# Queries computed by channels and rotated in that form, in a Mamba-2 and sliding-window attention trunk

## The chip, the cores and the metric

The kernel runs on one core of a Trainium2 chip. The metric is device time in microseconds for one launch. Before the change the median of three runs is 982.54 us (981.25 to 983.72). The trace shown below is of one more execution, which took 981.03 us.

## What is computed

The reference is a trunk of two layers on 256 tokens of 2048 channels, in float32. The first layer is a Mamba-2 mixer, the second a sliding-window attention. The change lies in the second layer alone, cut here to what matters:

```python
def _rope_partial(x, cos, sin):          # head dimension 64, the first 16 channels turn in pairs (i, i + 8)
    x1, x2, rest = xf[..., :8], xf[..., 8:16], xf[..., 16:]
    out = jnp.concatenate([x1 * cos - x2 * sin, x2 * cos + x1 * sin, rest], axis=-1)

def _swa_mixer(x, k, v, cos, sin, w_in, q_bias, sinks, w_out):
    proj = x @ w_in                                       # 256 x 2048 by 2048 x 4096
    q = (proj[..., :2048] + q_bias).reshape(1, 256, 4, 8, 64)
    gate = proj[..., 2048:]
    q = _rope_partial(q, ...)
    o = _swa_sink_attention(q, k, v, sinks)               # 4 key heads, 8 query heads each, window 128
    return (o * jax.nn.silu(gate)) @ w_out
```

The layer's output is added to the scaled input and normalised over the channels.

## The kernel before

**Products.** Every large product is made of three: a float32 operand is split into a rounded part (`wh`, `x1H`) and the rest (`wl`, `x1L`), and high by high, high by low and low by high are summed in one PSUM bank. Weights come from HBM in units of 128 x 2048 (two loads of 512 KB on SyncE's queue). ScalarE writes a unit's `wh` (L164) and VectorE its `wl` (L167), each in two halves of 1024 columns. There are four buffers for `wh` and four for `wl`, so a new unit's ScalarE piece has to wait until TensorE has read the unit four before it.

**Two forms.** In the form by tokens (`x_stat`, L1006) a tile of the input, 128 channels by 128 tokens, is stationary and 512 weight columns move; tokens come out on the partitions. One weight unit takes 24 such products, 12 for each half of the tokens. In the form by channels (`mac`, L252) a 128 x 128 tile of weights is stationary and all 256 tokens move; channels come out on the partitions. One weight unit takes 48 such products. In this second form a weight tile may lie *broken*: its first 128 columns apart from the rest, at another offset in the buffer (`BROKEN`, `BROKEN2`), and then the first half is written in two pieces.

**The second layer.** After keys and values (`kv`, form by tokens, two groups of transposes, L1063, turn the keys), twelve blocks of four weight units follow in the order of `B_ORDER`: query blocks `q` 0 to 3 (one key head each, 512 channels), gate blocks `g` 0 to 3 (form by channels), and output blocks `o` 0 to 3 (L323 to L325, 512 columns moving). Units of this layer are counted here from the first of `q` 0, so that `q` 0 is units 1 to 4, `g` 0 units 5 to 8, `q` 1 9 to 12, `g` 1 13 to 16, `q` 2 17 to 20, `o` 0 21 to 24, `g` 2 25 to 28, `q` 3 29 to 32, `o` 1 33 to 36, `g` 3 37 to 40, `o` 2 and `o` 3 after that.

**What runs between units.** `tick()` is called after each unit. `later(n, fn)` puts a piece of work on TensorE's list n units later. So a query block's transposes (`qtr`) come two units after it, its attention scores (`attend`, L1139 for the first 128 tokens) three units after it, the scores of the second half (L1146) three units later, and the products with the values (L1249, or L1263 and L1270) some units after those.

**A query block.** Two PSUM tiles, one for each half of the tokens, are filled over four units. VectorE adds the bias row (L1090, a row of 512 that GpSimd loads and spreads over the partitions, L981), turns the 16 rotary channels of each head (`rope`, six small operations, L991 to L996), TensorE transposes the 128 x 512 result into a PSUM tile (L1096, four transposes), and ScalarE copies it out with the factor 1/8 (L1100).

The engines run their own lists in order; within them the order comes from the program and a scheduler. ScalarE also makes the gates' tanh (L1116), the exponentials (L1174) and the moves of 32 x 256 pieces (L1207). VectorE also transposes the probabilities in 32 x 32 pieces (L1188) and applies the first layer's gains to the residual (L1028, L1029).

Of the kernel before, what the change touches and what calls it, by code (L numbers as in the profile page):

```python
# [8 lines left out]
F32 = mybir.dt.float32  # L9
# [74 lines left out]
def trunk(ctx: ExitStack, tc: tile.TileContext, A: dict, out: bass.AP, dbg=None):  # L84
    nc = tc.nc
# [8 lines left out]
    cst = pool("cst")  # L94
# [108 lines left out]
    srcs = []  # L203
# [11 lines left out]
    srcs += wo_srcs("wo", NG - 1) + [A["wkv"][i] for i in range(4)]  # L215
    places = {}
    for what, j in B_ORDER:
        if what == "g":

            places.update({len(srcs) + i: BROKEN2 if (i, j) == (1, 0) else BROKEN for i in range(4)})  # L220
        srcs += wo_srcs({"q": "wq", "g": "wg", "o": "wb"}[what], j)
    units = []
    used = [0]
# [34 lines left out]
    def later(n, fn, place=None):  # L258
        pending.insert(len(pending) if place is None else place, [n, fn])
# [528 lines left out]

    cs = cst.tile([P, 2, 8], F32, tag="cs", name="cs")
    sn = cst.tile([P, 2, 8], F32, tag="sn", name="sn")  # L790

    def rotary():
        posi = ap.tile([P, 2], I32, tag="posi", name="posi")
        tc.keep_in_program_order(nc.gpsimd.dma_start(posi[:], A["pos"]))
        inv = ap.tile([P, 8], F32, tag="inv", name="inv")
        tc.keep_in_program_order(nc.gpsimd.dma_start(inv[:], A["inv"]))
        posf = ap.tile([P, 2], F32, tag="posf", name="posf")
        nc.vector.tensor_copy(posf[:], posi[:])
        ang = ap.tile([P, 2, 8], F32, tag="ang", name="ang")
        nn = ap.tile([P, 2, 8], F32, tag="nn", name="nn")  # L800
        for h in range(2):
            nc.vector.tensor_scalar(ang[:, h, :], inv[:], posf[:, h : h + 1], None, ALU.mult)
        nc.vector.tensor_scalar(nn[:], ang[:], 1.0 / TWO_PI, None, ALU.mult)
        nc.vector.tensor_scalar(nn[:], nn[:], ROUND, None, ALU.add)
        nc.vector.tensor_scalar(nn[:], nn[:], ROUND, None, ALU.subtract)
        for c in (CW1, CW2, CW3):
            nc.vector.scalar_tensor_tensor(ang[:], nn[:], -c, ang[:], ALU.mult, ALU.add)
        nc.scalar.activation(sn[:], ang[:], AF.Sin)
        sh = ap.tile([P, 2, 8], F32, tag="sh", name="sh")
        nc.scalar.activation(sh[:], ang[:], AF.Sin, scale=0.5)  # L810
        nc.vector.tensor_tensor(sh[:], sh[:], sh[:], ALU.mult)
        nc.vector.tensor_scalar(cs[:], sh[:], -2.0, 1.0, ALU.mult, ALU.add)


    plan = {}
# [163 lines left out]
    def bias_row(src):  # L979
        t = bp.tile([P, 512], F32, tag="bias", name=nm("bias"), bufs=1)  # L980
        nc.gpsimd.dma_start(t[:], src.partition_broadcast(P))  # L981
        return t

    def rope(v, h, n):

        c = cs[:, h : h + 1, :].to_broadcast([P, n, 8])
        s = sn[:, h : h + 1, :].to_broadcast([P, n, 8])
        t = bp.tile([P, 4, 8, 8], F32, tag="rt", name=nm("rt"), bufs=1)
        x1, x2 = v[:, :, 0:8], v[:, :, 8:16]
        a, b, d, e = [t[:, i, :n, :] for i in range(4)]  # L990
        nc.vector.tensor_tensor(a, x1, c, ALU.mult)  # L991
        nc.vector.tensor_tensor(b, x2, s, ALU.mult)
        nc.vector.tensor_tensor(d, x2, c, ALU.mult)
        nc.vector.tensor_tensor(e, x1, s, ALU.mult)
        nc.vector.tensor_tensor(x1, a, b, ALU.subtract)
        tc.keep_in_program_order(nc.vector.tensor_tensor(x2, d, e, ALU.add))  # L996

    def x_stat(ps, h, u, ui, pin=False, last=None):

        todo = [(k, i) for k in range(4) for i in range(3) if i != last]  # L1000
        todo += [(k, last) for k in range(4) if last]
        for k, i in todo:
            kk = ui * 4 + k
            ks = slice(k * 512, (k + 1) * 512)
            hs = slice(h * P, (h + 1) * P)
            m = nc.tensor.matmul(  # L1006
                ps[:], (x1H, x1L, x1H)[i][:, kk, hs], (u.h, u.h, u.l)[i][:, ks],
                start=(kk, i) == (0, 0), stop=ui == 3 and (k, i) == todo[-1],
            )
            pinned(m, pin)  # L1010
# [19 lines left out]

    kT = bp.tile([P, 4, S], F32, tag="kT", name="kT")
    vt = bp.tile([P, 2, S], F32, tag="vt", name="vt")
    kvb = bias_row(A["kvb"])
    kv_u = []
    for h in range(2):
        ps = mm_tile()
# [34 lines left out]
    for i, n in enumerate(RES_AT):  # L1071
        later(n, lambda i=i: residual(i // 2, i % 2))

    qT = {}
    sg = {}
    os_ = {}
    still = []

    def q_block(j):
        pss = [mm_tile(), mm_tile()]  # L1080
        qb = bias_row(A["qb"][j * 512 : (j + 1) * 512])
        for ui in range(4):
            u = next_unit()
            for h in range(2):
                x_stat(pss[h], h, u, ui)
            tick()
        for h in range(2):
            qt = bp.tile([P, 8, 64], F32, tag="qt", name=nm("qt"), bufs=2)
            qf = qt[:].rearrange("p a d -> p (a d)")
            nc.vector.tensor_tensor(qf, pss[h][:], qb[:], ALU.add)  # L1090
            rope(qt[:], h, 8)

            def qtr(h=h, qf=qf):
                pt = ax_tile()
                for p_ in range(4):
                    nc.tensor.transpose(  # L1096
                        pt[:, p_ * P : (p_ + 1) * P], qf[:, p_ * P : (p_ + 1) * P], ident
                    )
                q2 = bp.tile([P, 4, P], F32, tag="qT", name=nm("qT"), bufs=2)
                nc.scalar.activation(  # L1100
                    q2[:], pt[:].rearrange("p (a t) -> p a t", a=4), AF.Copy, scale=0.125
                )
                qT[j, h] = q2

            later(2, qtr)

    def gate_block(j):
        t = bp.tile([P, 4, S], F32, tag="sg", name=nm("sg"), bufs=2)
# [12 lines left out]
    def attend(j, h):  # L1121

        nk = P * (h + 1)
        q2 = qT[j, h]
# [7 lines left out]
        for b in range(0, 4, per):  # L1132
            pss = [ax_tile(), ax_tile()]
            for i in range(per):
                for part in range(h + 1):
                    for par in range(2):
                        rows = slice(64 * par, 64 * par + 64)
                        if h == 0:
                            nc.tensor.matmul(  # L1139
                                pss[par][:, i * nk : (i + 1) * nk], q2[rows, b + i, :], kT[rows, j, :nk],  # L1140
                                start=True, stop=True,
                            )
                            continue

                        qs, at = slice(64 * part, 64 * part + 64), i * nk
                        nc.tensor.matmul(  # L1146
                            pss[par][qs, at : at + 192], q2[rows, b + i, qs],
                            kT[rows, j, 64 * part : 64 * part + 192], start=True, stop=True,
                        )
# [240 lines left out]
def _layout(inputs):  # L1390
# [44 lines left out]
    a["wkv"] = xstat(f["kv_w"], 4, 512)  # L1435
    a["kvb"] = f["kv_b"]
    wi = f["b_w_in"][0]
    a["wq"] = xstat(wi[:, :D], 4, 512)
    a["wg"] = wstat(wi[:, D:])
    a["qb"] = f["b_q_bias"][0]  # L1440
    a["snk"] = f["b_sinks"][0].reshape(4, 4, 2).transpose(0, 2, 1).reshape(32)
    wb = f["b_w_out"][0]
    a["wb"] = xstat(wb, 4, 512).reshape(4, 4, P, 2048).transpose(1, 0, 2, 3).reshape(16, P, 2048)
# [42 lines left out]
```

## Time and profile before

| | |
|---|---|
| median of the three runs | 982.54 us |
| profiled execution, its own time | 981.03 us |
| its span in the trace | 979.0 us |
| TensorE clock granted | 1.00 |
| bytes read from HBM | 195.49 MB, 202 GB/s over the span with the 2.23 MB written |
| keys and values begin, `q` 0 begins, `o` 2 begins | 655.59, 679.21, 923.59 us |

The profile counts a matmul as busy from its start to the modelled end of its flow through the array, and the next starts long before that end. So a row's duration (0.28 us for 256 columns) is no price. The price of a stretch is the distance from its first start to the next stretch's first start. A row of the timeline reads: start, duration, engine, line, operation, output and inputs, stationary and moving shapes, and how many operations were merged. `x1H` and `x1L` are the input of the second layer, `wh` and `wl` a weight unit, `mm` and `ax` PSUM tiles, `qt` the queries by tokens, `qT` the queries by channels, `kT` the keys by channels.

### The profile page before, as it was taken

The numbers are of one execution on the slowest core, as the hardware profiler recorded it, in microseconds if no ns is written. First come the engines' busy times: TensorE is split into PE (matmuls) and PEld (weight loads), VectorE is DVE, ScalarE is ACT, GpSimd is POOL, SyncE is SP. The second block draws the span as 40 slices with busy tenths as digits, with TensorE's granted clock in tenths as the row PEclk, the third lists the DMA queues.
The fourth block names the chain that finished last, engine by engine and source line by source line (L and its number), as shares of the span: only waits on it lengthen the run. The fifth ranks groups of instructions, "written<-read, shape, count | busy, mean of one in ns | idle before, by whom it ended". The sixth has DMA issues, their size and how long they took to land.

```text
span 979.0 us, 18089 instructions
## 1 busy us (share of the span) xinstructions
PE 973.5 (99%) x7012; PEld 884.5 (90%) x7012; DVE 783.3 (80%) x1201; ACT 660.7 (67%) x1222; POOL 98.7 (10%) x137
## 2 busy tenths in 40 slices
PE   9999999999999999999999999999999999999998
PEld 8999989999999998999999999888898878978976
DVE  7898898967888877886887787889867778766786
ACT  7595776764984865776576487566467777764772
POOL 0001303003003002100300300303000000000003
PEclk9999999999999999999999999999999999999999
DMA  9788577764665766666566565458645546564642
GB/s 356 267 289 305 171 223 230 237 201 145 222 221 173 258 207 190 217 202 206 187 212 204 170 203 199 152 166 291 214 153 175 181 162 187 166 210 142 203 142 86
DMA packets 61557, 198.89 MB, mean 203 GB/s; under 512 B 6848, under 2 KB 11360, under 8 KB 61216
## 3 DMA queue, kind: packets, MB, share of 16 engines
q1 hardware_dynamic: 58528, 188.53, 58.6%
q0 software_dynamic: 2336, 8.69, 2.7%
q8 instruction: 55, 0.90, 0.4%
q10 hardware_dynamic: 608, 0.52, 0.2%
q14 instruction: 30, 0.25, 0.1%
HBM read 195.49 MB, written 2.23 MB: 202 GB/s over the span
## 4 chain that ended last, share of the span: by engine, by line
PE 99%; DVE 0%; DVEq 0%; issue 0%
PE mm L252 54%; PE mm L1006 11%; PE mm L323 9%; PE mm L324 9%; PE mm L325 9%; PE ax L654 2%; PE ax L1146 1%; PE ax L1139 0%; PE ax L591 0%; PE mm L390 0%; PE ax L1263 0%; PE ax L1249 0%; PE ax L1096 0%; PE ax L937 0%; PE ax L372 0%; DVE t L1323 0%
## 5 line engine op out<-in xcount | busy, mean ns | idle before, releaser
L167 DVE TENSOR_TENSOR wl<-wr,wh 128x1024 fp32r<-128x1024 f32 (+2 forms) x338 | 392.9, 1180 | 87.9 <-ACT wh L164 84.5
L164 ACT ACTIVATE wh<-wr 128x1024 fp32r<-128x1024 f32 (+2 forms) x338 | 331.4, 1011 | 123.6 <-PE mm L252 63.2
L252 PE MATMUL mm<-xH,wh 128*128 128x256 f32 x1280 | 355.0, 277 | 0.0
L252 PE MATMUL mm<-xL,wh 128*128 128x256 f32 x1280 | 354.0, 277 | 0.0
L252 PE MATMUL mm<-xH,wl 128*128 128x256 f32 x1280 | 353.9, 276 | 0.0
L252 PEld LDWEIGHTS mm<-xH,wh 128*128 128x128 f32 x1280 | 240.6, 188 | 1.8 <-ACT wh L198 0.5
L252 PEld LDWEIGHTS mm<-xL,wh 128*128 128x128 f32 x1280 | 240.6, 188 | 1.0
L252 PEld LDWEIGHTS mm<-xH,wl 128*128 128x128 f32 x1280 | 240.4, 188 | 0.0
L323 PE MATMUL mm<-wh,yH 128*128 128x512 f32 x256 | 101.2, 395 | 0.0
L324 PE MATMUL mm<-wh,yL 128*128 128x512 f32 x256 | 99.8, 390 | 0.0
L325 PE MATMUL mm<-wl,yH 128*128 128x512 f32 x256 | 99.7, 389 | 0.0
L670 POOL TENSOR_TENSOR yz<-yz,z 128x256 f32<-128x256 f32 x32 | 26.8, 846 | 469.4 <-DVE yz L665 469.4
L494 DVE SCALAR_TENSOR_TENSOR cv<-mm,pc,cv 128x255 f32<-128x255 f32 x144 | 68.7, 477 | 5.2 <-ACT cv L492 2.6
L252 PE MATMUL mm<-x1H,wh 128*128 128x256 f32 x256 | 71.9, 281 | 0.0
L252 PE MATMUL mm<-x1L,wh 128*128 128x256 f32 x256 | 71.1, 278 | 0.0
L252 PE MATMUL mm<-x1H,wl 128*128 128x256 f32 x256 | 71.0, 278 | 0.0
L1006 PE MATMUL mm<-wh,x1H 128*128 128x512 f32 x160 | 63.1, 394 | 0.0
L1006 PE MATMUL mm<-wl,x1H 128*128 128x512 f32 x160 | 61.8, 389 | 0.0
L1006 PE MATMUL mm<-wh,x1L 128*128 128x512 f32 x160 | 60.9, 390 | 0.0
L323 PEld LDWEIGHTS mm<-wh,yH 128*128 128x128 f32 x256 | 48.1, 188 | 10.3 <-DVE z L584 0.9
L325 PEld LDWEIGHTS mm<-wl,yH 128*128 128x128 f32 x256 | 48.1, 188 | 10.2
L324 PEld LDWEIGHTS mm<-wh,yL 128*128 128x128 f32 x256 | 48.1, 188 | 9.0
(232 smaller groups left out, 1418.3 us busy)
## 6 DMA issues: line engine op xcount, KB each, us to landing
wr<-in_wa SPq DMA_DIRECT2D x154, 512.0 KB, 5.2
wr<-in_wo SPq DMA_DIRECT2D x64, 512.0 KB, 4.5
wr<-in_wq SPq DMA_DIRECT2D x32, 512.0 KB, 4.6
wr<-in_wg SPq DMA_DIRECT2D x31, 512.0 KB, 5.2
wr<-in_wb SPq DMA_DIRECT2D x16, 512.0 KB, 4.3
wr<-in_wb SPq DMA_DIRECT2D x32, 256.0 KB, 3.8
rb<-rscr SPq DMA_DIRECT2D x11, 512.0 KB, 5.7
wr<-in_wkv SPq DMA_DIRECT2D x8, 512.0 KB, 4.7
```

Source lines behind the costliest of these rows:

```text
L164: m = nc.scalar.activation(h[:, sl], v, AF.Copy)
L167: m = nc.vector.tensor_tensor(l[:, sl], v, h[:, sl].bitcast(F32), ALU.subtract)
L252: m = nc.tensor.matmul(ps, a, b, start=first and i == 0, stop=last and i == 2)
L323: pinned(nc.tensor.matmul(ps, aH[:, k, hs], u.h[:, ks], start=k == 0 and add is None, stop=False), pin)
L324: pinned(nc.tensor.matmul(ps, aL[:, k, hs], u.h[:, ks], start=False, stop=False), pin)
L325: pinned(nc.tensor.matmul(ps, aH[:, k, hs], u.l[:, ks], start=False, stop=k == 3), pin)
L494: nc.vector.scalar_tensor_tensor(a[:, sft:], ps[:, : S - sft], w(3 - sft), a[:, sft:], ALU.mult, ALU.add)
L654: nc.tensor.matmul(ps[64 * r : 64 * r + 64, cols], st.xd[:, c, i, 64 * r : 64 * r + 64], e[:, 256:] if c else e[:, :256], start=c == 0, st ...
L670: nc.gpsimd.tensor_tensor(v, v, st.z[i][:], ALU.mult)
L1006: m = nc.tensor.matmul(ps[:], (x1H, x1L, x1H)[i][:, kk, hs], (u.h, u.h, u.l)[i][:, ks], start=(kk, i) == (0, 0), stop=ui == 3 and (k, i) = ...
L1146: nc.tensor.matmul(pss[par][qs, at : at + 192], q2[rows, b + i, qs], kT[rows, j, 64 * part : 64 * part + 192], start=True, stop=True,)
```

## The change

Queries are computed in the form by channels, like the gates. Each of a block's four units gives one PSUM tile of 128 channels (two heads) by 256 tokens. ScalarE reads it out with 1/8 and the bias as a value per partition (the bias comes once as 128 x 16 and is scaled on GpSimd). For two such tiles at once, VectorE makes a copy in which channels 0 to 7 and 8 to 15 of each group of 32 partitions have changed places (stream shuffle), multiplies the tile by a map of cosines and ones, the copy by a map of sines and zeros, and adds them. The maps (`rot`, 128 channels by 256 tokens, twice) are made once: GpSimd lays out sine and cosine by tokens (`turned`, behind the rotary table in the first layer), and at the first tick of the second layer VectorE transposes that and ScalarE moves it into place in eight copies. The query units lie broken like those of the gates. Nothing is left for TensorE to transpose; `attend` reads slices of the new tiles.

```diff
-        if what == "g":
-            places.update({len(srcs) + i: BROKEN2 if (i, j) == (1, 0) else BROKEN for i in range(4)})
+        if what in "gq":
+            places.update({len(srcs) + i: BROKEN2 if (what, i, j) == ("g", 1, 0) else BROKEN for i in range(4)})
...
+        for i in range(2):
+            nc.gpsimd.memset(turned[:, :, i, 16:], 1.0 - i)
+            nc.gpsimd.tensor_copy(turned[:, :, 0, 8 * i : 8 * i + 8], cs[:])
+            nc.gpsimd.tensor_scalar(turned[:, :, 1, 8 * i : 8 * i + 8], sn[:], 2.0 * i - 1.0, None, ALU.mult)
...
+    rot = bp.tile([P, 2, S], F32, tag="rot", name="rot")
+    for k in range(2):
+        for i in range(2):
+            nc.gpsimd.memset(rot[64 * k + 32 : 64 * k + 64, i, :], 1.0 - i)
...
+    def rope_maps():
+        nc.gpsimd.tensor_scalar(qb[:], qb[:], 0.125, None, ALU.mult)
+        z = bp.tile([P, 2, 2, 32], F32, tag="rt", name="z", bufs=1)
+        nc.vector.transpose(z[:].rearrange("p h m t -> p (h m t)"), turned[:].rearrange("p h m t -> p (h m t)"))
+        for k in range(2):
+            lo = 64 * k
+            for a in range(4):
+                nc.scalar.copy(
+                    rot[lo : lo + 32].rearrange("p m (h a t) -> p a m h t", h=2, a=4)[:, a],
+                    z[32 * a : 32 * a + 32].rearrange("p h m t -> p m h t"),
+                )
+    later(1, rope_maps)
+    swap = [*range(8, 16), *range(8), *range(16, 32)]
...
     def q_block(j):
-        pss = [mm_tile(), mm_tile()]
-        qb = bias_row(A["qb"][j * 512 : (j + 1) * 512])
-        for ui in range(4):
+        qT[j] = []
+        for p_ in range(4):
             u = next_unit()
-            for h in range(2):
-                x_stat(pss[h], h, u, ui)
+            ps = mm_tile()
+            for k in range(KT):
+                mac(ps[:, :S], u.tile(0, k), u.tile(1, k), x1H[:, k, :], x1L[:, k, :], k == 0, k == KT - 1)
             tick()
-        for h in range(2):
-            qt = bp.tile([P, 8, 64], F32, tag="qt", name=nm("qt"), bufs=2)
-            qf = qt[:].rearrange("p a d -> p (a d)")
-            nc.vector.tensor_tensor(qf, pss[h][:], qb[:], ALU.add)
-            rope(qt[:], h, 8)
-            def qtr(h=h, qf=qf):
-                pt = ax_tile()
-                for p_ in range(4):
-                    nc.tensor.transpose(
-                        pt[:, p_ * P : (p_ + 1) * P], qf[:, p_ * P : (p_ + 1) * P], ident
+            if p_ % 2 == 0:
+                tag, n = (f"gb{p_ // 2}", 1) if j % 2 else ("qT", 2)
+                q = bp.tile([P, 2, S], F32, tag=tag, name=nm("qT"), bufs=n)
+                qT[j] += [q[:, 0], q[:, 1]]
+            i = j * 4 + p_
+            nc.scalar.activation(q[:, p_ % 2], ps[:, :S], AF.Identity, bias=qb[:, i : i + 1], scale=0.125)
+            if p_ % 2:
+                w = bp.tile([P, 2, S], F32, tag="qt", name=nm("sw"), bufs=2)
+                nc.vector.stream_shuffle(w[:].rearrange("p a t -> p (a t)"), q[:].rearrange("p a t -> p (a t)"), swap)
+                for v, m in ((q, 0), (w, 1)):
+                    nc.vector.tensor_tensor(
+                        v[:], v[:], rot[:, m : m + 1, :].to_broadcast([P, 2, S]), ALU.mult
                     )
-                q2 = bp.tile([P, 4, P], F32, tag="qT", name=nm("qT"), bufs=2)
-                nc.scalar.activation(
-                    q2[:], pt[:].rearrange("p (a t) -> p a t", a=4), AF.Copy, scale=0.125
-                )
-                qT[j, h] = q2
-            later(2, qtr)
+                nc.vector.tensor_tensor(q[:], q[:], w[:], ALU.add)
...
-    a["wq"] = xstat(wi[:, :D], 4, 512)
+    a["wq"] = wstat(wi[:, :D])
...
-    a["qb"] = f["b_q_bias"][0]
+    a["qb"] = f["b_q_bias"][0].reshape(16, P).T
```

Three places show how the engines' lists move. The first is TensorE at the end of `g` 0's second unit, before the change (`mm_8273` is that unit's PSUM tile, `mm_8350` the third's, `qt` the queries by tokens, `cc` holds the identity):

```order
L252 MATMUL mm_8273<-x1H,wh_8137 128x256
L252 MATMUL mm_8273<-x1L,wh_8137 128x256
L252 MATMUL mm_8273<-x1H,wl_8138 128x256
L1096 MATMUL ax_8324<-cc,qt_8175 128x128 x4
L1096 MATMUL ax_8331<-cc,qt_8184 128x128 x4
L252 MATMUL mm_8350<-x1H,wh_8194 128x256
L252 MATMUL mm_8350<-x1L,wh_8194 128x256
```

The same place in the changed kernel (the third unit's tile is `mm_8465`):

```order
L252 MATMUL mm_8400<-x1H,wh_8251 128x256
L252 MATMUL mm_8400<-x1L,wh_8251 128x256
L252 MATMUL mm_8400<-x1H,wl_8252 128x256
L252 MATMUL mm_8465<-x1H,wh_8321 128x256
L252 MATMUL mm_8465<-x1L,wh_8321 128x256
```

The eight transposes are gone and the two units touch. The second place is TensorE where keys and values (`mm_7940`) end and the first query unit begins, before:

```order
L1006 MATMUL mm_7940<-wh_7813,x1L 128x512
L1006 MATMUL mm_7940<-wl_7814,x1H 128x512
L1006 MATMUL mm_8009<-wh_7835,x1H 128x512
L1006 MATMUL mm_8009<-wh_7835,x1L 128x512
L1006 MATMUL mm_8009<-wl_7836,x1H 128x512
```

And there in the changed kernel, where the first query tile is `mm_8039`:

```order
L1011 MATMUL mm_7958<-wh_7827,x1L 128x512
L1011 MATMUL mm_7958<-wl_7828,x1H 128x512
L252 MATMUL mm_8039<-x1H,wh_7849 128x256
L252 MATMUL mm_8039<-x1L,wh_7849 128x256
L252 MATMUL mm_8039<-x1H,wl_7850 128x256
```

One product of 512 columns has become two of 256; everything else on TensorE's list keeps its place, unit by unit. The third place is VectorE after the last unit of `q` 0, before (`mm_8009` holds the first half of the tokens, `rt` scratch, `gb` a row of gains):

```order
L1090 TENSOR_TENSOR qt_8175<-mm_8009,bias_8011 128x512
L1028 TENSOR_TENSOR xr<-xr,gb_947_8003 128x512
L991 TENSOR_TENSOR rt_8177<-qt_8175,cs 128x64
L992 TENSOR_TENSOR rt_8177<-qt_8175,sn 128x64
L993 TENSOR_TENSOR rt_8177<-qt_8175,cs 128x64
L994 TENSOR_TENSOR rt_8177<-qt_8175,sn 128x64
L1029 TENSOR_TENSOR xr<-xr,gb_947_8003 128x512
L995 TENSOR_TENSOR qt_8175<-rt_8177 128x8x8
L996 TENSOR_TENSOR qt_8175<-rt_8177 128x8x8
```

And in the changed kernel (`qT_8249` are the third and fourth unit's queries, `sw` the shuffled copy, `wl` pieces of weight units to come):

```order
L1119 STREAM_SHUFFLE sw_8315<-qT_8249 128x512
L167 TENSOR_TENSOR wl_8389<-wr_8390,wh_8388 128x896
L1121 TENSOR_TENSOR qT_8249<-qT_8249,rot 128x512
L1121 TENSOR_TENSOR sw_8315<-sw_8315,rot 128x512
L167 TENSOR_TENSOR wl_8389<-wr_8392,wh_8388 128x1024
L1124 TENSOR_TENSOR qT_8249<-qT_8249,sw_8315 128x512
L1033 TENSOR_TENSOR xr<-xr,gb_947_8024 128x512
```

Seven operations for each half of the tokens have become four for each pair of tiles, among the same weight pieces and residual operations. SyncE's list of loads is the same in both kernels.

More of the change, by code (lines that the diff above doesn't have):

```diff
@@ L790, in trunk @@
     sn = cst.tile([P, 2, 8], F32, tag="sn", name="sn")
+    turned = cst.tile([P, 2, 2, 32], F32, tag="map", name="map")
     def rotary():
@@ L977, in trunk @@
     nc.gpsimd.dma_start(snk, A["snk"].partition_broadcast(P))
[L979 to L982, printed above, removed]
+    rot = bp.tile([P, 2, S], F32, tag="rot", name="rot")
+    for k in range(2):
+        for i in range(2):
+            nc.gpsimd.memset(rot[64 * k + 32 : 64 * k + 64, i, :], 1.0 - i)
     def rope(v, h, n):
@@ L1032, in trunk @@
     vt = bp.tile([P, 2, S], F32, tag="vt", name="vt")
-    kvb = bias_row(A["kvb"])
+    kvb = bp.tile([P, 512], F32, tag="qT", name="kvb", bufs=2)
+    nc.gpsimd.dma_start(kvb[:], A["kvb"].partition_broadcast(P))
+    qb = bp.tile([P, 16], F32, tag="qb", name="qb")
+    nc.gpsimd.dma_start(qb[:], A["qb"])
     kv_u = []
@@ L1123, in attend, with q2 @@
         nk = P * (h + 1)
-        q2 = qT[j, h]
+        def q2(rows, i, q0, n):
+            return qT[j][i][rows, h * P + q0 : h * P + q0 + n]
         p = bp.tile([P, 1024], F32, tag="p", name=nm("p"), bufs=3)
@@ L1139, in attend @@
                             nc.tensor.matmul(
-                                pss[par][:, i * nk : (i + 1) * nk], q2[rows, b + i, :], kT[rows, j, :nk],
+                                pss[par][:, i * nk : (i + 1) * nk], q2(rows, b + i, 0, P), kT[rows, j, :nk],
                                 start=True, stop=True,
@@ L1146, in attend @@
                         nc.tensor.matmul(
-                            pss[par][qs, at : at + 192], q2[rows, b + i, qs],
+                            pss[par][qs, at : at + 192], q2(rows, b + i, 64 * part, 64),
                             kT[rows, j, 64 * part : 64 * part + 192], start=True, stop=True,
```

## The prediction

> **What bounds the kernel now.** I read the page first: the engines' busy time, the clock, the chain that ended last. Then what TensorE waited for, then stretches of its timeline.
>
> ```profile
> PE 973.5 (99%) x7012; PEld 884.5 (90%) x7012; DVE 783.3 (80%) x1201; ACT 660.7 (67%) x1222; POOL 98.7 (10%) x137
> PEclk9999999999999999999999999999999999999999
> PE 99%; DVE 0%; DVEq 0%; issue 0%
> ```
>
> TensorE is busy 99% of the span at the full clock in all 40 slices, and the chain runs on it almost alone. A busy row may hide idle cycles, so the waits of TensorE come next (engine, line, waited for: total, times, longest).
>
> ```profile
> PE ax L372 <- DVE zero L360: 1.0, 1, 1.0
> ```
>
> One microsecond at the start is all the waiting of the whole program. So a change is worth what it takes from or adds to TensorE's own list, as long as nothing new makes it wait. The weights are ready early, which the busiest ScalarE group shows:
>
> ```profile
> L164 ACT ACTIVATE wh<-wr 128x1024 fp32r<-128x1024 f32 (+2 forms) x338 | 331.4, 1011 | 123.6 <-PE mm L252 63.2
> ```
>
> ScalarE sat idle 123.6 us before these pieces, and over half of that until TensorE had freed a weight buffer: it waits for TensorE, not the other way round.
>
> **The pace of the two forms.** The change replaces 4 x 96 = 384 products of 512 columns by 768 of 256. The first row below is three query units in the form by tokens (it counts one product too many, which began before; 3 x 24 = 72), the others are gate units in the form by channels (from, to, us, busy and count of matmuls and of weight loads, clock, DMA).
>
> ```profile
> 679.21:695.54 16.33, 16.33 (x73) 13.33 (x71) 1.00 0.88 300
> ...
> 701.87:712.79 10.92, 10.92 (x96) 10.88 (x95) 1.00 0.58 183
> 713.59:719.41 5.82, 5.82 (x48) 5.69 (x48) 1.00 0.66 214
> 749.59:755.13 5.54, 5.54 (x48) 5.42 (x47) 1.00 0.31 95
> 840.05:851.27 11.22, 11.22 (x96) 11.18 (x96) 1.00 0.47 142
> 912.58:923.59 11.01, 11.01 (x96) 10.98 (x96) 1.00 0.56 176
> 7.91:20.82 12.91, 12.91 (x108) 12.78 (x108) 1.00 1.04 410
> ```
>
> By tokens: 16.33 / 3 = 5.44 us a unit, 226.8 ns a product. By channels: 10.92 / 2 = 5.46 us a unit, 113.75 ns a product. So two small products cost 227.5 ns against 226.8 ns for one large one. 384 x 0.7 ns = 0.3 us is the most that the form as such costs; part of the 0.7 ns is how the two stretches begin and end. I take **+0.1 us**, bounds 0 and 0.3.
>
> The form by channels has a second, slower pace, though. The stretch from 840.05 and that from 912.58 are alike (two gate units behind the scores L1146), and the first is 11.22 - 11.01 = 0.21 us longer; the unit from 713.59, behind transposes, takes 5.82. In all these rows the slow pace begins behind another kind of matmul, and in the pair from 840.05 it lasts for one unit of the two. Near the program's start 108 products took 12.91 us, 119.5 ns each, the dearest row that this form has.
>
> **What TensorE loses.** The transposes stand at four places, behind gate units in `q` 0 and 1, among output units in `q` 2 and 3 (start, duration, then as above):
>
> ```profile
> 712.79 1.04 PE L1096 MATMUL ax<-cc,qt 128*128 128x128 f32 x8
> 713.59 0.36 PE L252 MATMUL mm<-x1H,wh 128*128 128x256 f32 x1
> ...
> 812.50 1.03 PE L1096 MATMUL ax<-cc,qt 128*128 128x128 f32 x8
> 813.29 0.48 PE L323 MATMUL mm<-wh,oH 128*128 128x512 f32 x1
> 813.60 0.40 PE L324 MATMUL mm<-wh,oL 128*128 128x512 f32 x1
> ```
>
> Behind a gate unit the eight transposes hold the list from 712.79 to 713.59, 0.80 us. The unit behind them takes 5.82 us; the unit from 749.59, which like it ends before an attention piece but begins right behind another unit, takes 5.54. So 0.28 us more goes: 1.08 us a place, 2.16 for two. Among output units it is 813.29 - 812.50 = 0.79 us, and the first product behind takes 813.60 - 813.29 = 0.31 us instead of 0.227, 0.08 more: 0.87 a place, 1.74 for two. All of it lies on the path, since TensorE never waits there. Removed: 2.16 + 1.74 = **3.90 us**.
>
> **What TensorE gains beside the form.** Five of the sixteen query units come right behind a matmul of another kind: unit 4 behind the keys' transposes, units 11 and 19 behind the scores L1146, unit 18 behind L1263 and L1270, unit 32 behind L1249. As products of 512 columns they didn't have the slow pace; now they may. In the rows, units behind transposes were slow (713.59), of those behind L1146 one had a slow unit and one not. I count three of five slow: 3 x 0.21 = **+0.6 us**, bounds 0 and 1.05. The slow gate unit of the stretch from 840.05 and another beside it may also fall out otherwise, 0.4 us either way.
>
> **What the other engines get.** Their busy time between the first query unit and `o` 2, and in the densest part for ScalarE, is this (TensorE, weight loads, VectorE, ScalarE, GpSimd):
>
> ```profile
> 679.21:923.59 244.38, 244.38 (x1637) 211.31 (x1636) 184.00 (x322) 163.70 (x380) 5.64 (x8) 1.00 0.57 181
> 726.00:749.00 23.00, 23.00 (x129) 18.68 (x128) 14.66 (x28) 19.76 (x60) 0.00 (x0) 1.00 0.49 160
> ```
>
> The prices of what they do come from these groups (busy, mean ns of one):
>
> ```profile
> L1090 DVE TENSOR_TENSOR qt<-mm,bias 128x512 f32<-128x512 f32 x8 | 5.4, 676 | 0.5 <-PE mm L1006 0.5
> L996 DVE TENSOR_TENSOR qt<-rt 128x64 f32<-128x64 f32 x8 | 1.7, 216 | 0.0
> L1188 DVE STREAM_TRANSPOSE z<-p 128x1024 f32<-128x1024 f32 x8 | 9.9, 1237 | 0.0
> L625 DVE STREAM_TRANSPOSE zx<-xs 128x256 f32<-128x256 f32 x28 | 12.0, 437 | 0.9
> L1100 ACT ACTIVATE qT<-ax 128x512 f32<-128x512 f32 x8 | 4.4, 585 | 0.0
> L1116 ACT ACTIVATE sg<-mm 128x256 f32<-128x256 f32 x16 | 5.9, 368 | 0.0
> L1207 ACT COPY pt<-z 32x256 f32<-32x256 f32 x40 | 16.1, 404 | 1.3 <-DVE z L1188 0.8
> L167 DVE TENSOR_TENSOR wl<-wr,wh 128x1024 fp32r<-128x1024 f32 x306 | 372.1, 1232 | 83.7 <-ACT wh L164 80.7 <-DMA wr<-in_wb 0.3
> L167 DVE TENSOR_TENSOR wl<-wr,wh 128x896 fp32r<-128x896 f32 x15 | 16.3, 1086 | 1.9 <-ACT wh L164 1.6
> L167 DVE TENSOR_TENSOR wl<-wr,wh 128x128 fp32r<-128x128 f32 x15 | 4.2, 279 | 2.3 <-ACT wh L164 2.3
> ```
>
> VectorE loses 8 x (0.676 + 6 x 0.216) = 15.8 us. It gets 8 x (a shuffle of 512 columns + 3 x 0.676). No shuffle is in the trace; the stream transposes of 256 and 1024 columns, 0.44 and 1.24 us, bound it, and I take 0.7, in between: 8 x 2.73 = 21.8 us. Breaking 16 units adds 16 x (0.279 + 1.086 - 1.232) = 2.1. In all +8 us in 244, of which it worked 184. The Trainium skill ("VectorE: DVE Perf Modes", the perf-mode tier table) gives a shuffle about 2400 ns for 2048 elements; an estimate from that page is 0.6 us for 512, and as the work is hidden the sum stays the same with it.
>
> ScalarE loses 8 x 0.585 = 4.7 us and gets 16 read-outs of 128 x 256 (0.368 to 0.585: 5.9 to 9.4), eight copies for the maps at 0.4 or less (3.2) and the broken units' pieces, which I put at VectorE's 2.1. That is +7 to +10 in 244, of which it worked 164. In the dense part four units' read-outs and pieces add 2.0 to 2.9 us to 19.76 of 23, which still fits. With four buffers the weights are prepared up to three units ahead, so a short backlog is made up in the next stretch. GpSimd, with 5.64 us of work in 244, has room for its memsets and few map operations. SyncE's loads are the same bytes in the same order. Cost of all this: nothing. The cover is the lead of the weights; without it, what was late would be paid one to one.
>
> The new wait is VectorE's for ScalarE's read-out. Behind it on VectorE's list stand weight pieces for units to come, and those who wait for the result are the scores L1139, three units (16.4 us) after the block. The path to them is one read-out (0.59), one shuffle (0.7), three products (2.0) and the two weight pieces that the order puts between them (1.09 + 1.23): 5.6 us. Over ten are left.
>
> For the first query unit the cover is shorter, since its weights are prepared while VectorE is loaded by the keys:
>
> ```profile
> 672.35 4.85 DVE L167 TENSOR_TENSOR wl<-wr,wh 128x1024 fp32r<-128x1024 f32 x4
> ...
> 679.21 0.39 PE L1006 MATMUL mm<-wh,x1H 128*128 128x512 f32 x1
> ```
>
> Four pieces, the first two query units', are done by 677.20, the first unit's two by about 674.9; the unit begins at 679.21. Two broken pieces add 0.3 us there. It holds.
>
> **The sum.** -3.90 + 0.1 + 0.6 = -3.2 us. The profiled execution took 981.03 us with a span of 979.0, so its own time would be 977.8. It lies 1.5 us under the median of the three runs, 982.54; the forecast against that median is **979.3 us**. The bounds of this case: -3.9 - 0.4 = -4.3 (978.2), and -3.9 + 0.3 + 1.05 = -2.55 (980.0).
>
> **The rivals.** First, *the form by channels is dearer in the query units than in the gates*, for instance all sixteen in the slow pace: 16 x 0.21 = 3.4 instead of 0.6, so -3.9 + 0.1 + 3.4 = -0.4 (982.1). At the pace near the start, 768 x (119.5 - 113.75) ns = 4.4 us, it is +0.6 (983.1). For it: the rows of the slow pace. Against it: the gate units that begin right behind another unit, those from 701.87 and 749.59 among them, don't show it, one of them right behind a query unit, and the query tiles will lie in the same buffers at the same offsets. The Trainium skill ("TensorE: Matmul & The Clock Gate", Back-to-back issue gap) has a rule of this kind, a fixed 2.5 ns for each matmul beside its columns. By that rule 384 more matmuls cost 0.96 us, which would bring the gain to some 2.3 us, 980.2; the trace does not bear it out, with 0.7 ns for a pair at most. Chance 0.13.
>
> Second, on the other side: *the scores wait for the queries*. Place: TensorE before L1139, four times. It decides from the point where the queries come later than 16.4 us after their block. To turn the sum to slower by 0.3%, TensorE must wait 3.2 + 2.95 = 6.2 us, 1.5 at each place, so the path must take 18 us in place of 5.6. If the read-outs or the shuffles get stuck behind softmax work so that it takes 20, it costs 4 x 3.6 = 14.4 us: 993.7. For it: ScalarE's 19.76 of 23 us in the dense part, and lists that run in order. Against it: ten us of room, and the gates' read-outs stand in the same lists today without a wait of TensorE. Chance 0.12, with all milder amounts of waiting that end above the median.
>
> Third, *the transposes were hidden anyway*, and nothing changes: 982.5. The waits of TensorE speak against it. Chance 0.03.
>
> **The numbers.** The forecast's own case has 0.72. About 0.3%, 2.95 us, is what a measurement of this kernel can tell from no change; the forecast passes that by only 0.25, with four or five slow units it doesn't. Of the 0.72 I put 0.55 on faster and 0.17 on within; with the two rivals within (0.13 and 0.03) that makes 0.33. Slower has 0.12. The range reaches from 978.0 to 983.0: the forecast's bounds and the first rival, without the second.
>
> **What would show it.** Right: no L1096 on TensorE, no new row among its waits, the stretch from the first query unit to `o` 2 about 241.2 us instead of 244.38, three or so query units at 5.7 us and the others at 5.46, ScalarE and VectorE each some 8 us busier. Wrong: TensorE waiting for `qT` at the scores or for `wh`, query units at 5.65 or more throughout, or the time between 679 and 924 unchanged.

## The result: 1.6 us faster, half of what was forecast

| | before | after |
|---|---|---|
| median (lowest to highest) | 982.74 us (981.25 to 986.38), 20 runs | 981.12 us (980.37 to 982.95), 20 runs |
| ratio after / before, 95% interval | | 0.9986 [0.998, 0.9992] |
| span of the profiled execution | 979.0 us | 978.6 us |
| `q` 0 begins, `o` 2 begins | 679.21, 923.59 us | 679.82, 921.70 us |
| last output product done | 970.63 us | 969.76 us |

The gain is real, but at 0.14% [0.08, 0.2] it lies within the 0.3% that counted as no change. Lines of the kernel after are about 5 to 21 higher: keys and values are L1011, the scores L1160 and L1167 (L1139 and L1146 before), the products with the values L1270, L1284 and L1291, the gating of their result L1258 (L1237 before), the queries' read-out L1116.

The page of after, its first row and the chain that ended last, and what TensorE waited for:

```profile
PE 972.5 (99%) x7364; PEld 896.7 (92%) x7364; DVE 789.4 (81%) x1202; ACT 666.5 (68%) x1254; POOL 103.2 (11%) x145
PE 90%; DVE 5%; ACT 2%; issue 1%; DMA 1%; DVEq 0%; ACTq 0%
```

```profile
PE ax L372 <- DVE zero L360: 1.0, 1, 1.0
```

TensorE's products still wait for nothing but their first operand, and VectorE and ScalarE have 6 us more to do. The chain leaves TensorE more than before (90% instead of 99%), but up to the last output product it does so only ahead of 145 us, in the first layer, which the change hardly touches. In the second layer the change acts through TensorE's list alone. Stretches of after, TensorE alone (from, to, us, busy and count, clock, DMA): first query unit to `o` 2, the first three query units, one query unit behind the products with the values, the first unit of `o` 0 and of `o` 1, the first two of `o` 2, the last output products.

```profile
679.82:921.70 241.88, 241.88 (x1990) 1.00 0.55 178
679.82:696.18 16.36, 16.36 (x145) 1.00 0.79 270
780.61:786.46 5.85, 5.85 (x52) 1.00 0.49 143
799.14:804.83 5.69, 5.69 (x27) 1.00 0.21 74
872.75:878.44 5.69, 5.69 (x28) 1.00 0.65 212
921.70:932.99 11.29, 11.29 (x51) 1.00 0.75 279
941.39:969.76 28.37, 28.37 (x139) 1.00 0.13 47
```

The same of before: the query unit that stood at the place of the third row, then the places of the fourth, sixth and seventh.

```profile
782.17:787.86 5.69, 5.69 (x29) 1.00 0.72 235
800.37:805.90 5.53, 5.53 (x25) 1.00 0.31 100
923.59:934.59 11.00, 11.00 (x50) 1.00 0.77 287
942.88:970.63 27.75, 27.75 (x139) 1.00 0.12 44
```

The stretch with the queries is 2.50 us shorter (244.38 to 241.88), and the query units cost 16.36 / 3 = 5.45 us as forecast. But the output units, which the change doesn't touch, are dearer: 11.29 for 11.00 us, 28.37 for 27.75, 5.69 for 5.53. The step between two starts of an output product is 231 or 236 ns by turns, 233 on average, instead of 227. Over `o` 0 to `o` 3 that is about 2.1 us, half of it inside the stretch before `o` 2.

What the other engines got, by groups of after (busy, mean ns of one, idle before):

```profile
L1116 ACT ACTIVATE qT<-mm,qb 128x256 f32<-128x256 f32 x16 | 7.4, 460 | 0.1
L1119 DVE STREAM_SHUFFLE sw<-qT 128x512 f32<-128x512 f32 x8 | 6.0, 745 | 0.0
L1121 DVE TENSOR_TENSOR qT<-qT,rot 128x512 f32<-128x512 f32 x8 | 5.5, 686 | 0.0
L1121 DVE TENSOR_TENSOR sw<-sw,rot 128x512 f32<-128x512 f32 x8 | 5.5, 684 | 0.0
L1124 DVE TENSOR_TENSOR qT<-qT,sw 128x512 f32<-128x512 f32 x8 | 5.5, 685 | 0.0
L1090 ACT COPY rot<-z 32x128 f32<-32x128 f32 x8 | 2.4, 296 | 1.4 <-DVE z L1086 1.3
```

The operations on VectorE cost what was forecast within 0.05 us each, and ScalarE's read-outs and copies lie inside their bounds. And the program's last stores, two of the DMA groups from 960 us on (KB each, median us to landing), of before and then of after:

```profile
q14 instruction: 1, 0.01, 0.1%
out<-xr SPq DMA_DIRECT2D x3, 128.0 KB, 1.9
```

```profile
q14 instruction: 2, 0.02, 0.2%
out<-xr SPq DMA_DIRECT2D x3, 128.0 KB, 2.4
```

From the last output product to the end of the span before took 8.37 us and after 8.85, 0.48 more: three small stores land later, beside one more packet on the instruction queue `q14`.

### The profile page after: what moved, and what is told of

Same layout as the page of the kernel before. It is cut to its first block, busy times and chain, and to the rows that moved or that the text cites. A ratio compares the mean times of both kernels' runs of the same rounds, so it can differ in the third digit from the quotient of the medians.

```text
span 978.6 us, 18818 instructions
## 1 busy us (share of the span) xinstructions
PE 972.5 (99%) x7364; PEld 896.7 (92%) x7364; DVE 789.4 (81%) x1202; ACT 666.5 (68%) x1254; POOL 103.2 (11%) x145
## 4 chain that ended last, share of the span: by engine, by line
PE 90%; DVE 5%; ACT 2%; issue 1%; DMA 1%; DVEq 0%; ACTq 0%
PE mm L252 56%; PE mm L323 9%; PE mm L324 9%; PE mm L325 9%; PE mm L1011 2%; PE ax L654 2%; DVE wl L167 1%; ACT e L550 1%; DVE cv L494 1%; DMA rb<-rscr 1%; PE ax L1167 1%; DMA wr<-in_wa 1%; ACT wh L164 1%; PE ax L1160 0%; PE mm L390 0%
## 5 line engine op out<-in xcount | busy, mean ns | idle before, releaser
L252 PE MATMUL mm<-x1H,wh 128*128 128x256 f32 x512 | 143.0, 279 | 0.0
L252 PE MATMUL mm<-x1L,wh 128*128 128x256 f32 x512 | 141.8, 277 | 0.0
L252 PE MATMUL mm<-x1H,wl 128*128 128x256 f32 x512 | 141.7, 277 | 0.0
L252 PEld LDWEIGHTS mm<-x1H,wh 128*128 128x128 f32 x512 | 96.1, 188 | 3.9 <-issue 2.4
L252 PEld LDWEIGHTS mm<-x1L,wh 128*128 128x128 f32 x512 | 96.4, 188 | 0.1
L252 PEld LDWEIGHTS mm<-x1H,wl 128*128 128x128 f32 x512 | 96.2, 188 | 0.0
```

Of the source, the lines that this page charges most:

```text
L252: m = nc.tensor.matmul(ps, a, b, start=first and i == 0, stop=last and i == 2)
```

## The experiments

**Why the output products are slower.** In the layout of the built programs a tile's address within a partition, modulo 256 bytes, is 0 for `wh` in both kernels. `oH` and `oL` lie at 0 before and at 64 after, because the new bias tile `qb` takes 64 bytes ahead of them. Theory: the pace depends on where the two operands lie to each other. Rival: other work (a busier VectorE and ScalarE, the weights' loads) slows these products.

**E1: the bias tile takes 256 bytes instead of 64**, so that all later tiles lie as before.

```diff
-    qb = bp.tile([P, 16], F32, tag="qb", name="qb")
+    qb = bp.tile([P, 64], F32, tag="qb", name="qb")[:, :16]
```

> The changed kernel, with the bias tile qb given 256 bytes a partition instead of 64 (16 of 64 columns are used), so that all tiles laid out after it begin at 0 modulo 256 bytes again, as they did before the change. Theory A (the output blocks lost their pace because oH and oL moved by 64 bytes): the products of L323 to L325 in o 0 to o 3 go back from about 235 to 227 ns, from the first query unit to the end 2.2 us less than in the changed kernel, a ratio to the kernel before of about 0.996. Rival B (the output blocks are slower because VectorE and ScalarE are busier beside them, or because of what runs before them): nothing changes, 233 to 236 ns, ratio about 0.9985.

Measured: 979.23 us (7 runs) against 982.14 before (30 runs), ratio 0.9972 [0.9959, 0.9985]. Stretches of it, the first from the first query unit to `o` 2, the others output units:

```profile
679.09:920.47 241.38, 241.38 (x1989) 1.00 0.56 179
798.62:804.18 5.56, 5.56 (x27) 1.00 0.19 63
920.47:931.47 11.00, 11.00 (x50) 1.00 0.75 287
939.76:967.51 27.75, 27.75 (x139) 1.00 0.13 46
```

The output units are back at 11.00 and 27.75, with all of the new work on VectorE and ScalarE in place, and the rival falls. By the starts of its units, `o` 0 takes 22.25 us in E1 and 22.79 in after, `o` 1 22.27 and 22.78, `o` 2 and `o` 3 44.42 and 45.45: 0.54 + 0.51 + 1.03 = 2.08 us.

**E2: the kernel before, with an unused tile of 64 bytes behind the bias row.**

```diff
+    gap = bp.tile([P, 16], F32, tag="gap", name="gap")
+    nc.gpsimd.memset(gap[:], 0.0)
```

> The kernel before, with nothing but an unused tile of 64 bytes a partition behind the bias row, cleared once by GpSimd; oH and oL begin at 64 modulo 256 bytes. Theory A: the output blocks' products go from 227 to about 235 ns, some 2.2 us longer, ratio about 1.002. Rival B: 227 ns and no difference, ratio 1.000.

Measured: 983.98 us (12 runs), ratio 1.0015 [1.0004, 1.0025]. Its stretches: the gate unit behind the queries' transposes, then output units.

```profile
715.96:721.60 5.64, 5.64 (x51) 1.00 0.60 193
802.37:808.06 5.69, 5.69 (x26) 1.00 0.36 102
926.70:937.99 11.29, 11.29 (x51) 1.00 0.76 280
946.39:974.76 28.37, 28.37 (x139) 1.00 0.10 39
```

64 bytes that nobody reads give the kernel before exactly the output units of after: 5.69, 11.29, 28.37. The unit behind the transposes has 5.64 instead of 5.82: the shift also moved the transposed tile, and the slow pace behind it went.

**E3: the kernel before without its 32 transposes**; ScalarE copies the unturned queries. It measures what the transposes cost, by itself.

```diff
-                pt = ax_tile()
-                for p_ in range(4):
-                    nc.tensor.transpose(
-                        pt[:, p_ * P : (p_ + 1) * P], qf[:, p_ * P : (p_ + 1) * P], ident
-                    )
...
-                    q2[:], pt[:].rearrange("p (a t) -> p a t", a=4), AF.Copy, scale=0.125
+                    q2[:], qf.rearrange("p (a t) -> p a t", a=4), AF.Copy, scale=0.125
```

> The kernel before, with the 32 transposes of the queries left out: ScalarE copies the untransposed queries instead of the transposed ones, everything else stands. It measures the removed term by itself. The prediction's step: 3.9 us less, of which 1.1 at each of the two places behind gate units and 0.87 at each of the two among output units, ratio 0.996. If the transposes had been hidden: ratio 1.000. If the slow pace of a gate unit doesn't hang on the transposes before it: 3.3 to 3.5 us.

Measured: 978.37 us (11 runs), ratio 0.9965 [0.9953, 0.9978]. Its stretch from the first query unit to `o` 2:

```profile
680.18:920.63 240.45, 240.45 (x1605) 1.00 0.57 184
```

244.38 - 240.45 = 3.93 us; the forecast had 3.90.

**E5: E1 with the query units' weights unbroken.**

```diff
-        if what in "gq":
+        if what in "g":
```

> The changed kernel with qb at 256 bytes and the query units' weights not broken (all 16 tiles of a unit in a row), the gates' as they are. If breaking has no effect on the pace: like the run with qb at 256 bytes, query units at 5.46 us. If breaking is what lets a unit settle into the fast pace: query units at 5.65 us or more, up to 16 x 0.2 = 3.2 us longer than that run.

Measured: 983.09 us (10 runs), ratio 1.0009 [0.9998, 1.002]. Its stretch from the first query unit to `o` 2, and the first three query units:

```profile
679.72:924.93 245.21, 245.21 (x1989) 1.00 0.56 176
679.72:696.99 17.27, 17.27 (x146) 1.00 0.76 253
```

17.27 / 144 = 119.9 ns a product instead of 16.36 / 144 = 113.6, and 3.83 us more in the stretch: that eats the whole gain. The break moves 15 of a unit's 16 weight tiles by 64 bytes against the input. So the form's price is decided by an address here too.

**E8 and E9: `oH` and `oL` at 128 and at 192** (the bias tile of after takes 128 bytes in E8, as below, or 192 in E9).

```diff
-    qb = bp.tile([P, 16], F32, tag="qb", name="qb")
+    qb = bp.tile([P, 32], F32, tag="qb", name="qb")[:, :16]
```

> The changed kernel with qb at 128 bytes a partition: oH and oL begin at 128 modulo 256. Theory A1 (any offset other than the weights' costs pace): output products at 235 ns. Theory A2 (only some offsets do): 227 ns.

> The changed kernel with qb at 192 bytes a partition: oH and oL begin at 192 modulo 256. Theory A1: output products at 235 ns. Theory A2: 227 ns, or a pace of its own.

Measured: 980.34 and 978.89 us (one run each). Output stretches of E8 and, behind it, of E9:

```profile
921.33:932.58 11.25, 11.25 (x51) 1.00 0.76 280
940.97:969.27 28.30, 28.30 (x139) 1.00 0.11 42
```

```profile
920.69:931.77 11.08, 11.08 (x51) 1.00 0.76 285
940.08:967.99 27.91, 27.91 (x139) 1.00 0.13 49
```

At 128 the loss is nearly that at 64 (28.30 for 28.37), at 192 a quarter of it (27.91). So neither one slow pace for all offsets nor a fast one for some describes it: each offset has a pace of its own.

**E10: E1 with 64 bytes ahead of the weight buffers**, so that `oH`, `oL` and `wh` all lie at 64 and `x1H` at 0. It tells the absolute place from the distance.

```diff
+    gap = cst.tile([P, 16], F32, tag="gap", name="gap")
+    nc.gpsimd.memset(gap[:], 0.0)
```

> The changed kernel with qb at 256 bytes and a gap of 64 bytes ahead of the weight buffers, so that oH, oL and the weights all begin at 64 modulo 256, while the second layer's input x1H and x1L stays at 0. If the distance between the two operands sets the pace (theory D): the output products stay at 227 ns, and the gate and query units, whose distance has changed by 64, lose pace, up to 0.3 us each. If the place of the stationary operand alone sets it: output products at 235 ns, gate and query units as before.

Measured: 986.53 us (one run). Its stretches: 60 products of keys and values (weights moving), three query units, output units.

```profile
666.83:680.66 13.83, 13.83 (x63) 1.00 0.77 230
680.66:697.81 17.15, 17.15 (x145) 1.00 0.79 266
804.51:810.06 5.55, 5.55 (x26) 1.00 0.37 108
928.40:939.40 11.00, 11.00 (x50) 1.00 0.82 285
```

With both operands at 64 the output units are fast, and keys and values, whose weights now lie 64 from the input, take 229 ns a step instead of 227: the distance decides, not the place of one operand. And the units whose weights now lie otherwise against `x1H` are slow: 17.15 for 16.36.

**The slow units.** In after, four units of gates and queries keep a pace of 118 ns instead of 113: 18, 19, 26 and 27. The last two were slow before the change. In E1 they are 4, 18, 19 and 26. Theory: such a unit follows the offset of the small tiles that the matmuls ahead of it read. Rival: the weights' own place decides.

**E11: the small tiles of the attention (keys, values, queries and, but for `pte`, which lies at 0, the probabilities) at 64, `oH` and `oL` at 0.** The `qb` of after moves ahead of the sinks, and a gap of 192 bytes follows the keys.

```diff
+    qb = bp.tile([P, 16], F32, tag="qb", name="qb")
...
-    qb = bp.tile([P, 16], F32, tag="qb", name="qb")
...
+        if h == 0:
+            gap = bp.tile([P, 48], F32, tag="gap", name="gap")
+            nc.gpsimd.memset(gap[:], 0.0)
```

> The changed kernel with qb's 64 bytes ahead of the sinks' tile and a gap of 192 bytes behind the tiles of keys and shuffled queries: keys, values, queries by channels, the keys by tokens kd and the probabilities' tiles begin at 64 modulo 256, the exponentials, pte, oH and oL at 0. Theory A: the output blocks keep 227 ns. Theory C, from four runs (the unit behind the keys' or queries' transposes is slow where the transposed tile begins at 0, and not where it begins at 64): unit 4 is fast, 0.2 us less than in the run with qb at 256 bytes; if the same holds for keys and values, the units behind the scores and the products with the values (18, 19, 26, 27) turn fast too, 0.8 us more. Ratio to the kernel before 0.996 to 0.997. Rival: the slow units come and go without regard to offsets, and the same units stay slow.

Measured: 979.55 us (11 runs), ratio 0.9969 [0.9956, 0.9981]. Units 4 and 18 in E11, and unit 4 in E1:

```profile
697.09:702.60 5.51, 5.51 (x51) 1.00 0.48 149
780.73:786.59 5.86, 5.86 (x53) 1.00 0.45 130
```

```profile
696.25:701.96 5.71, 5.71 (x51) 1.00 0.41 140
```

Half right: unit 4, behind the keys' transposes, becomes fast, as the gate units behind transposes did in E2; in E8 and E9, with the transposed tile at 128 and 192, it is fast too. Units 18, 19, 26 and 27 stay slow.

**E12: E1 with the other break for units 18, 19, 26 and 27** (two tiles of 128 columns apart from the rest instead of one).

```diff
-            places.update({len(srcs) + i: BROKEN2 if (what, i, j) == ("g", 1, 0) else BROKEN for i in range(4)})
+            places.update({len(srcs) + i: BROKEN2 if (what, i, j) == ("g", 1, 0) or (j == 2 and i in (1, 2)) else BROKEN for i in range(4)})
```

> The changed kernel with qb at 256 bytes, and with the units 18, 19, 26 and 27, the slow ones behind attention products, broken after two tiles instead of one (BROKEN2). If a break at another place lets them settle into the fast pace: 5.66 instead of 5.85 us at 18 and 26, up to 0.8 us less than the run with qb at 256 bytes, ratio to the kernel before about 0.996. If the slow pace there doesn't hang on the break: no difference, 0.997.

Measured: 979.96 us (11 runs), ratio 0.9975 [0.9965, 0.9985]: no better than E1. Unit 18, units 19 and 20, unit 26, and what TensorE waited for at the scores behind unit 26:

```profile
782.16:787.82 5.66, 5.66 (x52) 1.00 0.42 125
789.28:800.50 11.22, 11.22 (x101) 1.00 0.41 139
832.00:837.66 5.66, 5.66 (x52) 1.00 0.14 22
```

```profile
PE ax L1167 <- DVE o L1258: 0.4, 1, 0.4
```

Units 18 and 26 gain 0.19 us each, unit 19 stays slow (11.22 with unit 20), and unit 27 was fast in E1 already. The gain is given back at one place: the scores L1167 last 2.44 us instead of 1.46, since they need a PSUM tile that VectorE hasn't read yet. VectorE's list there, of before and then of after (start, duration):

```profile
833.92 0.74 DVE L1237 TENSOR_TENSOR o<-ax,sg 128x256 f32<-128x256 f32 x2
```

```profile
835.76 1.21 DVE L167 TENSOR_TENSOR wl<-wr,wh 128x1024 fp32r<-128x1024 f32 x1
836.89 0.74 DVE L1258 TENSOR_TENSOR o<-ax,sg 128x256 f32<-128x256 f32 x2
```

Before, that operation ended at 834.66, 3.9 us ahead of the scores (838.59). After, it ends at 837.63 and the scores begin at 837.03, so only their second half, which comes later, still finds it done. Where TensorE's list is quicker up to there, it waits: 0.54 us in E1 (scores 2.00 instead of 1.46), 0.98 in E12.

**E13: E1 without the shuffles and the three operations behind them**, the queries staying unturned.

```diff
-            if p_ % 2:
-                w = bp.tile([P, 2, S], F32, tag="qt", name=nm("sw"), bufs=2)
-                nc.vector.stream_shuffle(w[:].rearrange("p a t -> p (a t)"), q[:].rearrange("p a t -> p (a t)"), swap)
-                for v, m in ((q, 0), (w, 1)):
...
-                nc.vector.tensor_tensor(q[:], q[:], w[:], ALU.add)
```

> The changed kernel with qb at 256 bytes, with the shuffles and the products with the maps left out, so that the queries are not rotated: 32 VectorE operations less. The prediction's step (VectorE's work costs nothing): no difference to the run with qb at 256 bytes, 241.4 us from the first query unit to o 2, and VectorE some 22 us less busy. If it were on the path: up to 22 us less.

Measured: 978.66 us (5 runs), ratio 0.9972 [0.996, 0.9984], the same as E1's. First query unit to `o` 2 in E13 and in E1, all engines (TensorE, weight loads, VectorE, ScalarE, GpSimd):

```profile
681.18:922.21 241.03, 241.03 (x1990) 223.99 (x1988) 174.74 (x280) 169.29 (x409) 2.77 (x4) 1.00 0.56 179
```

```profile
679.09:920.47 241.38, 241.38 (x1989) 223.85 (x1988) 191.56 (x320) 169.23 (x408) 2.76 (x4) 1.00 0.56 179
```

VectorE has 16.8 us less in this stretch (22 were expected), and TensorE's stretch is 0.35 us shorter. That is E1's wait of 0.54 gone, less 0.19 because unit 27, fast in E1, is slow again. The wait alone doesn't make that unit fast: in E11 the scores last 1.94 us, and unit 27 is slow.

Two cautions. The profiled executions reach the first query unit at different times: E1's 0.1 us ahead of before's, the others 0.2 (E9) to 2.4 us (E2) behind it. Most of that is stalls in the first layer (near 6, 135 and 269 us), in kernels with and without the change; so traces are compared by stretches of the second layer, and kernels by medians. By themselves the spans of before and after differ by 0.4 us alone: +0.61 up to the first query unit, -1.48 from there to the last output product, +0.48 behind it. And E8 to E10 have one time each; only their stretches are used.

## Why the prediction was right or wrong

From the first query unit to the end of the last output product the profiled executions took 291.42 us before (679.21 to 970.63), 289.94 after, 288.42 in E1. The steps, in us:

| step of the prediction | forecast | after | E1 |
|---|---|---|---|
| transposes removed | -3.90 | -3.93 (E3) | -3.93 |
| the form as such | +0.1 | about 0.0 | about 0.0 |
| query units in the slow pace | +0.6 | +0.32 | +0.52 |
| a gate unit's pace (27) | 0, 0.4 either way | 0 | -0.19 |
| other engines | 0 | 0 | +0.54 |
| output blocks | not listed | +2.08 | 0 |
| sum | -3.2 | -1.5 | -3.1 |
| measured in this stretch | | -1.48 | -3.00 |

**What bounds the kernel: right.** TensorE waits nowhere new in after, and VectorE's added 6 us (7.9 between the first query unit and `o` 2, where +8 was forecast) cost nothing. E13 takes 16.8 us from VectorE and gains 0.35. ScalarE was given too much: in the same stretch it works 169.48 us instead of 163.70, 5.8 more where 7 to 10 were forecast, which cost nothing either.

**The transposes: right,** 3.93 for 3.90, although of two different kinds: E2 shows that 0.18 of the 1.08 us at a gate unit hung on the offset of the transposed tile.

**The form: right, by a condition the prediction named in half a sentence.** Two units take 11.00 or 11.01 us in either form, as the rows of `o` 2 and of the gates (912.58 before) show. The Trainium skill's fixed 2.5 ns for each matmul ("TensorE: Matmul & The Clock Gate", Back-to-back issue gap), which that section gives for an isolated matmul and by which 384 more would cost an estimated 0.96 us, isn't seen: what E3 leaves between it and after, 241.88 - 1.05 in output blocks - 240.45 = 0.38, is taken up by two slow units to 0.06. The prediction took the gates' price for the queries because "the query tiles will lie in the same buffers at the same offsets"; E5 shows that all hangs on that. Without the break the first rival would have come true, near its dearer variant, which gave +0.6 us: E5's stretch is 0.83 us longer than before's. That the totals agree to 0.01 us (983.1 and 983.09) is luck, since that sum started from 982.54 and E5 was run beside a median of 982.14. The cause differs too: E5's units step by 120 ns at distance 0, while the row near the program's start that priced the variant steps by 118 at a distance of 192, which elsewhere goes at 113.

**The slow units: kind right, size half.** Three of five at 0.21 were forecast. Two came, 18 and 19, at 5.85 - 5.69 = 0.16 each, since the units that they replace weren't at the best price either. E1 has unit 4 as well, with 0.20.

**What failed: the sum.** It ran over what the diff removes, adds and moves on TensorE, and gave every other product its old price. A tile of 64 bytes that GpSimd scales once shifted the stationary operands of the 384 output products, and each lost 5 ns: +2.08 us, two thirds of the forecast gain. The trace of before could not show it; the layout of the built program could, and the prediction looked at offsets only for the queries. With E1's 256 bytes the gain is 2.9 us (979.23 against 982.14) for the 3.2 forecast.

**Two smaller misses.** The cover on VectorE was judged at the first scores (L1160), three units behind a block, and there it holds. It is thin at the second scores behind unit 26: VectorE's lead shrank from 3.9 us to less than nothing, and whatever makes TensorE quicker ahead of it is partly given back (E12). And the tail: after, E1 and the six other kernels with broken query units have two packets on the queue `q14` beside the last stores, which land in 2.2 to 2.7 us; before, E2, E3 and E5 have one, and 1.9 to 2.0. Twelve traces agree, about 0.5 us of the total, but no experiment isolated it.

**What stays open:** why units 18, 19, 26 and 27 fall into the slow pace. The other break frees 18 and 26, not 19; the small tiles' offset doesn't free them. Why the distance matters at all is not known either.

The chances: 0.33 stood on within 0.3%, where it ended, made up of a milder forecast (0.17), the first rival and hidden transposes. The cause was none of these. The measured 981.12 lies above the forecast's own bounds (978.2 to 980.0); that it lies within the stated range is luck, since the range reached that far for the first rival's sake. The best versions measured are E11, 0.9969 [0.9956, 0.9981] against the kernel before, and E1, 0.9972 [0.9959, 0.9985], which these intervals don't tell apart.

## What to carry to other kernels

When a change adds or resizes a tile, compare the addresses of all later tiles, not only of those in the diff: in a kernel bound by TensorE, 64 bytes were worth 2.1 us and one line of padding brought them back. Price a matmul group by operands that lie as its own will lie, and repeat the price for groups that the change only shifts. Before speeding up TensorE's list further, look where another engine's lead is shortest; here a gain of 0.38 us was lost at one such place.

## What the runs showed of the hardware

The pace of a long run of matmuls with float32r operands depends on the distance in memory of the moving operand from the stationary one, within a partition and modulo 256 bytes:

| moving minus stationary | 512 columns moving, mean step in ns | 256 columns moving, mean step in ns |
|---|---|---|
| 0 | 227 (before, E1, E10) | 120 (E5) |
| 64 | 229 (E9; keys and values in E10) | not run |
| 128 | 232.5 (E8) | 119 (E10) |
| 192 | 233 (after, E2) | 113 (after, E1, the first layer) |

The first layer's input lies at 192 and its `wh` at 0, in after `x1H` at 0 and most of `wh` at 64: other places, the same distance, and the same 113 ns. So the two forms want different distances: 0 is best for the weights moving in 512 columns and worst for the weights stationary. The number of columns seems to decide that, not which operand is the weight: the last output products, 256 weight columns at distance 0, also step by 120 ns (before, from 967.51 us on; these are only 24, and in after, at 192, they step by 118). The Trainium skill ("SBUF — State Buffer", Operand start alignment) treats an operand's start as a matter of legality and says that its runs timed nothing; here it has a price of 1 to 3% at 512 columns and 5 to 6% at 256.

A run of matmuls can also keep a slower pace for one whole unit (48 products, 118 ns instead of 113) after matmuls of another kind, and then lose it at the next unit. Near the program's start one kept it for 108 products (7.91 to 20.82 in before). Which tile the matmuls ahead read, by its offset, settled it for units behind transposes (unit 4: 5.71 us with that tile at 0, 5.51 at 64, and about as little at 128 and 192 in E8 and E9), not for those behind the attention.
